# Attention stage of a Mamba-2 and stick-breaking trunk: when the gate, the flips and the transposes run, and on which PSUM banks

## The chip, the cores and the metric

One Trainium2 chip, one core of it. The metric is the time of one execution on the device in microseconds (us), the median of several. Five engines work side by side, each through a queue of its own in order: TensorE (PE in the rows; PEld is its loading of stationary operands), VectorE (DVE), ScalarE (ACT), GpSimd (POOL) and SyncE (SP, which issues the DMAs). Matmuls write to PSUM, eight banks of 512 floats in each of 128 partitions.

## The reference

The reference is a decoder trunk of two layers over 1024 positions of width 1024: a Mamba-2 layer, then a stick-breaking attention layer with 16 heads of 64. The change is in the second layer alone. There the queries, a gate and the shared keys and values are projected, keys and queries are normalised per head, and each block of 128 queries is combined with the keys before it:

```python
z = jnp.einsum('bhtd,bhsd->bhts', q[:, :, q0:kend], k[:, :, :kend])
log_keep = jnp.where(strict, jax.nn.log_sigmoid(-z), 0.0)
suffix = lax.cumsum(log_keep, axis=3, reverse=True) - log_keep
weights = jnp.where(strict, jnp.exp(jax.nn.log_sigmoid(z) + suffix), 0.0)
...
outs.append(jnp.einsum('bhts,bhsd->bhtd', weights, v[:, :, :kend]))
...
return (o * jax.nn.silu(gate)) @ w_out
```

The kernel computes the weights as differences of a running product of sigmoid(-z), which one scan gives, and multiplies them by differences of neighbouring values.

## The kernel before

All large products are made in three passes of a reduced float type: each operand is split in a high half (rounded, by ACT) and a low half (the rest, by DVE or POOL), and high x high, high x low and low x high are added in PSUM.

`attention` goes through 8 head pairs `hp` and, in each, through 4 pairs of 128-row blocks, p = 3, 2, 1, 0: 32 steps, and two more at the end. Positions are stored in reverse, so block pair p = 3 sees the fewest keys and p = 0 the most. Step i mixes three kinds of work:

- **fill** for `steps[i]`: `project` of the blocks 2p+1 and 2p (24 matmuls of 384 columns each: keys, values and queries), and in the steps p = 3 and p = 2 `gate` of one half of the positions (24 matmuls of 512 columns). The generators give way (`yield`) every so many matmuls, and the pieces below are put in there. A list of weights (5, 7, 5) turns the count of yields into a position between 0 and 1.
- **pieces for `steps[i-1]`**: `flip` (L873) transposes its normalised keys and queries into one PSUM bank `tq` (L879) and splits them into `kst`, `qh` and `ql` by ACT and DVE (L885 to L890). Then `scores` makes z for two heads and two blocks (L906, L907), ACT takes sigmoid(-z) (L908), and DVE's scan makes the running product `pt` (L910).
- **pieces for `steps[i-2]`**: `turn` transposes blocks of `pt` (L922, L925) into a `tr` bank and splits them into `wh` (ACT, L931) and `wl` (DVE, L932). `product` multiplies them by the values into `oq` (L942), two turns behind. `fold` reads `oq` by ACT and DVE (L953, L954), adds, and multiplies by the gate `GT` (L959).

So in a step p the pieces are the scores of block pair p+1 and the products of p+2 (of the pair before where that runs over). The number of turns is 6, 8, 2 and 4 in the steps p = 3, 2, 1 and 0; the keys that the scores reach are 896 and 1024, 128 and 256, 384 and 512, 640 and 768.

After the fill of a step come `values` (DMAs on SP that shift the values by one row, then POOL) and `norm` (sum of squares, twelve small DVE operations, one multiply of `kq`). The weights of the next pair are split into halves by ACT and DVE (L104, L108) as soon as their buffers come free. They come free when the last fill of p = 0 has read them.

The order of PE is the order in which the code issues. Only PE is scheduled by hand (`manual_schedule`); the order of the other engines is made by the planner of the framework, which also puts the waits in. The PSUM banks of the stage are `mm` 2, `z` 2, `tr` 2 and `oq` 2. In the last steps `b2.weights` loads the output weights and splits them, the low halves in turn on POOL and DVE. Steps 32 and 33 have as their fill the first output products (`b2.fill`, L1116).

```python
SPREAD = ((0.05, 0.95), (0.62, 1.0))
FLIP = 0.5
...
yield from split3_some(nc, ps[:, :384], prs, 6)
...
fill = [(project(sts[hp], 2 * p + 1), 5)]
if p >= 2:
    fill.append((gate(sts[hp], p - 2), 7))
fill.append((project(sts[hp], 2 * p), 5))
...
for f, w in fill:
    for _ in f:
        done += 1
        while pieces and pieces[0][0] <= done / total:
            pieces.pop(0)[1]()
```

## Time and profile before

| | us |
|---|---|
| median of 3 runs | 1828.4 (1828.0 to 1832.74) |
| the profiled execution | 1827.5 |
| its span, first to last instruction | 1825.8 |
| attention, from its first projection to the first output product | about 654 (927.4 to 1581.8) |

Over the whole span PE is busy 94%, DVE 65%, ACT 49% and POOL 22%. Shares of the span are averages over stages with different limits; in the attention stage DVE is far busier than in the rest. The profile gives each instruction its engine, its line in the kernel, the tiles it writes and reads (out<-in), its shape, start and duration, and where an engine sat idle in front of it, for how long and what ended that. Matmuls are pipelined: the duration of one is longer than the distance to the next, and the distance is what counts.

### The profile page before, as it was taken

How to read it: one execution, taken by the hardware profiler on the slowest of the kernel's cores; microseconds unless marked ns; L12 is line 12 of the kernel's file. 1: busy time of each engine (PE TensorE's matmuls, PEld its weight loads, DVE VectorE, ACT ScalarE, POOL GpSimd, SP SyncE). 2: the span in 40 equal slices, each digit the busy share in tenths (PEclk: the TensorE clock that was granted, in tenths of full speed). 3: DMA queues.
4: the chain of work that ended last, by engine and by line, in shares of the span. 5: the costliest groups of instructions: out<-in, count | busy, mean ns of one | idle time of the engine just before them, and what ended most of it. 6: DMA issues, size and time to landing. Idle time of an engine off the chain costs nothing.

```text
span 1825.8 us, 25280 instructions
## 1 busy us (share of the span) xinstructions
PE 1719.5 (94%) x9170; PEld 1449.3 (79%) x9170; DVE 1186.9 (65%) x2462; ACT 893.0 (49%) x1912; POOL 406.1 (22%) x450
## 2 busy tenths in 40 slices
PE   7999999999999999999998999998999998789999
PEld 6777877877886877888887888887888887677887
DVE  6687278179169645335659787978878787764332
ACT  6567349339337433123436464655646564642121
POOL 0234534624625122210001010111111012211110
PEclk9999999999999999999999999999999999899999
DMA  4222213213212655322211110101101011323110
GB/s 156 66 82 84 90 58 99 87 56 96 102 53 88 218 160 173 104 98 79 83 65 49 37 53 20 54 20 51 43 28 56 29 41 37 122 76 116 51 39 35
DMA packets 96397, 139.42 MB, mean 76 GB/s; under 512 B 18160, under 2 KB 66640, under 8 KB 96272
## 3 DMA queue, kind: packets, MB, share of 16 engines
q1 hardware_dynamic: 96272, 137.80, 23.5%
q8 instruction: 72, 1.18, 0.3%
q14 instruction: 53, 0.43, 0.1%
HBM read 108.77 MB, written 24.77 MB: 73 GB/s over the span
## 4 chain that ended last, share of the span: by engine, by line
PE 69%; DVE 19%; ACT 6%; DMA 3%; issue 2%; POOL 1%; SPq 0%; DVEq 0%; POOLq 0%; ACTq 0%
PE mm L46 37%; PE mm L53 12%; DVE pt L910 6%; PE mm L1116 4%; PE pq L46 2%; PE oq L942 2%; DVE v L234 2%; PE intra L409 2%; DVE g0l L108 1%; PE tr L922 1%; PE inter L404 1%; DVE wl L932 1%; PE tr L664 1%; PE tr L925 1%; PE tr L388 1%
## 5 line engine op out<-in xcount | busy, mean ns | idle before, releaser
L46 PE MATMUL mm<-ul,wh 128*128 128x512 f32 (+1 forms) x648 | 254.0, 392 | 0.0
L46 PE MATMUL mm<-uh,wl 128*128 128x512 f32 (+1 forms) x648 | 252.5, 390 | 0.0
L46 PE MATMUL mm<-uh,wh 128*128 128x512 f32 (+1 forms) x648 | 252.4, 389 | 0.1
L53 PE MATMUL mm<-g0h,hh 128*128 128x384 f32 x512 | 182.7, 357 | 0.0
L910 DVE TENSOR_TENSOR_SCAN pt<-pt,keep 128x128 f32<-128x128 f32 (+7 forms) x128 | 175.8, 1376 | 0.9 <-ACT pt L908 0.3
L53 PE MATMUL mm<-g0l,hh 128*128 128x384 f32 x512 | 172.8, 338 | 2.4 <-DVE g0l L108 2.4
L53 PE MATMUL mm<-g0h,hl 128*128 128x384 f32 x512 | 173.0, 338 | 0.0
L931 ACT CAST wh<-tr 128x512 fp32r<-128x512 f32 (+1 forms) x160 | 86.7, 543 | 165.0 <-PE tr L925 164.3
L234 DVE SCALAR_TENSOR_TENSOR v<-u,convh,v 128x512 f32<-128x512 f32 x144 | 129.4, 904 | 55.1 <-ACT v L232 52.6
L853 POOL TENSOR_TENSOR vs<-vs,vr 128x256 f32<-128x256 f32 x32 | 24.8, 776 | 548.5 <-DMA vs<-vr 265.9
L46 PEld LDWEIGHTS mm<-ul,wh 128*128 128x128 f32 x648 | 121.7, 188 | 26.2 <-issue 2.3
L46 PEld LDWEIGHTS mm<-uh,wh 128*128 128x128 f32 x648 | 121.7, 188 | 25.7 <-issue 1.1
L46 PEld LDWEIGHTS mm<-uh,wl 128*128 128x128 f32 x648 | 121.8, 188 | 25.5 <-issue 1.9
L932 DVE TENSOR_TENSOR wl<-tr,wh 128x512 fp32r<-128x512 f32 (+1 forms) x160 | 101.5, 635 | 55.6 <-ACT wh L931 53.5
L106 POOL TENSOR_TENSOR wl<-raw,wh 128x1024 fp32r<-128x1024 f32 x39 | 95.2, 2441 | 156.2 <-ACT wh L104 156.2
L574 DVE SCALAR_TENSOR_TENSOR acc<-mm,rg,acc 128x512 f32<-128x512 f32 x64 | 47.8, 749 | 84.5 <-PE mm L46 84.0
L53 PEld LDWEIGHTS mm<-g0l,hh 128*128 128x128 f32 x512 | 96.9, 189 | 3.9 <-DVE g0l L108 3.0
L53 PEld LDWEIGHTS mm<-g0h,hh 128*128 128x128 f32 x512 | 96.7, 189 | 1.0
L53 PEld LDWEIGHTS mm<-g0h,hl 128*128 128x128 f32 x512 | 96.4, 188 | 0.0
L922 PE MATMUL tr<-ident,pt 128*128 128x128 f32 x320 | 74.0, 280 | 23.5 <-DVE wl L932 22.3
L906 PE MATMUL z<-kst,qh 128*128 128x320 f32 (+3 forms) x192 | 72.2, 376 | 25.3 <-ACT pt L908 16.4
L908 ACT ACTIVATE pt<-z 128x320 f32<-128x320 f32 (+3 forms) x192 | 89.7, 489 | 8.9 <-PE z L907 7.4
(368 smaller groups left out, 4286.7 us busy)
## 6 DMA issues: line engine op xcount, KB each, us to landing
raw<-in_w_in SPq DMA_DIRECT2D x40, 512.0 KB
ex<-acd SPq DMA_DIRECT2D x64, 256.0 KB
raw<-in_w_b SPq DMA_DIRECT2D x32, 512.0 KB
raw<-in_m_out SPq DMA_DIRECT2D x16, 512.0 KB
raw<-in_gate SPq DMA_DIRECT2D x16, 512.0 KB
graw<-gT SPq DMA_DIRECT2D x30, 256.0 KB
gT<-zs SPq DMA_DIRECT2D x28, 256.0 KB
acc<-in_x SPq DMA_DIRECT2D x8, 512.0 KB
```

The source lines that it names most:

```text
L46: nc.tensor.matmul(out, lhsT=a, rhs=b, start=(i == 0), stop=(i == n - 1))
L53: nc.tensor.matmul(out, lhsT=a, rhs=b, start=(i == 0), stop=(i == n - 1))
L106: (eng or nc.gpsimd).tensor_tensor(lo, raw, hi.bitcast(F32), op=ALU.subtract)
L234: nc.vector.scalar_tensor_tensor(vv, u[:, 3 - j:3 - j + 512], w(j), vv, op0=ALU.mult, op1=ALU.add)
L574: nc.vector.scalar_tensor_tensor(acc[:, sl], ps, k.rg[:, g, t:t + 1], acc[:, sl], op0=ALU.mult, op1=ALU.add)
L906: nc.tensor.matmul(z[:, :n], lhsT=qh[:, h, qs], rhs=rk, start=True, stop=False)
L908: nc.scalar.activation(pt[:, ko:ko + n], z[:, :n], AF.Sigmoid, scale=-1.0)
L910: nc.vector.tensor_tensor_scan(pt[:, :N], pt[:, :N], keep[:, :N], 1.0, op0=ALU.mult, op1=ALU.max)
L922: nc.tensor.transpose(tq[:, c:c + P], al[:, i0:i0 + P], ident)
L931: nc.scalar.copy(wh[:, :c], tq[:, :c])
L932: nc.vector.tensor_tensor(wl[:, :c], tq[:, :c], wh[:, :c].bitcast(F32), op=ALU.subtract)
L1116: nc.tensor.matmul(pss[n], lhsT=a, rhs=b, start=(q == 0 and i == 0), stop=(q == 1 and i == 11))
```

## The change

Six things change, all in `attention` but the last:

- The gate moves from the steps p = 3 and p = 2 to p = 1 (between the two projections) and p = 0 (behind them); in the last pair to p = 2 and p = 1.
- The fill gives way every two matmuls (before: six in a projection, four in a gate), and the weights (12 each) match the number of yields.
- The flip moves from 0.5 to 0.58 of a step, the scores begin at 0.66 for 0.62. The flip writes keys and queries to two banks, and its ACT and DVE operations are put in another order.
- The transposes have three banks, and the products of both heads share one bank `oqs`, 256 columns each, which stays allocated.
- The copy of the values out of PSUM goes from DVE to ACT.
- In `B2.weights` all low halves are made by POOL.

```diff
-SPREAD = ((0.05, 0.95), (0.62, 1.0))
-FLIP = 0.5
+SPREAD = ((0.05, 0.95), (0.66, 1.0))
+GATE = {1: 1, 0: 0}
+GATE7 = {2: 1, 1: 0}
+FLIP = 0.58
...
-        trp = ctx.enter_context(tc.tile_pool(name="b_tr", bufs=2, space=PSUM, reuse_waits="tile"))
-        op = ctx.enter_context(tc.tile_pool(name="b_o", bufs=2, space=PSUM, reuse_waits="tile"))
+        trp = ctx.enter_context(tc.tile_pool(name="b_tr", bufs=3, space=PSUM, reuse_waits="tile"))
+        op = ctx.enter_context(tc.tile_pool(name="b_o", bufs=1, space=PSUM, reuse_waits="tile"))
...
+        oqs = op.tile([P, 512], F32, name="oq")
...
         def project(st, b):
-            yield from split3_some(nc, ps[:, :384], prs, 6)
+            yield from split3_some(nc, ps[:, :384], prs, 2)
...
-            nc.vector.tensor_copy(st["vr"][p][:, b % 2], ps[:, 128:256])
+            nc.scalar.copy(st["vr"][p][:, b % 2], ps[:, 128:256])
...
         def gate(st, half):
-            yield from split3_some(nc, gp, prs, 4)
+            yield from split3_some(nc, gp, prs, 2)
...
         def flip(st, p):
-            tq = trp.tile([P, 512], F32, name="tr")
-            for i in range(2):
-                for m in range(2):
-                    nc.tensor.transpose(tq[:, m * 256 + i * P:m * 256 + (i + 1) * P], kn[:, i, m], ident)
-            kt, qt = tq[:, 0:256], tq[:, 256:512]
+            kt, qt = (trp.tile([P, 512], F32, name="tr")[:, :256] for _ in range(2))
+            for m, t in ((0, kt), (1, qt)):
+                for i in range(2):
+                    nc.tensor.transpose(t[:, i * P:(i + 1) * P], kn[:, i, m], ident)
             qh = wk.tile([P, 2, 256], F32R, name="qh", bufs=1)
             for h in range(2):
+                o = own[h]
+                nc.scalar.activation(kst[o, h, tsl], kt[o], AF.Copy, scale=k.gkq[o])
+            for h in range(2):
                 o, x = own[h], own[1 - h]
-                g = k.gkq[o]
-                nc.scalar.activation(kst[o, h, tsl], kt[o], AF.Copy, scale=g)
                 nc.vector.scalar_tensor_tensor(
-                    kst[x, h, tsl], kt[o], g, kst[o, h, tsl].bitcast(F32), op0=ALU.mult, op1=ALU.subtract)
+                    kst[x, h, tsl], kt[o], k.gkq[o], kst[o, h, tsl].bitcast(F32), op0=ALU.mult, op1=ALU.subtract)
+            for h in range(2):
+                o, x = own[h], own[1 - h]
                 nc.scalar.copy(qh[o, h], qt[o])
                 nc.scalar.copy(qh[x, h], qt[o])
+            for h in range(2):
+                o = own[h]
                 nc.vector.tensor_tensor(ql[o, h], qt[o], qh[o, h].bitcast(F32), op=ALU.subtract)
...
         def product(st, p, h, j0):
-            if j0 == 2 * p:
-                st["oq"] = op.tile([P, 512], F32, name="oq")
-            out = st["oq"][:, :256]
+            out = oqs[:, h * 256:h * 256 + 256]
...
         def fold(st, p, h):
-            hp, GT, oq = st["hp"], st["GT"], st["oq"]
+            hp, GT, oq = st["hp"], st["GT"], oqs[:, h * 256:h * 256 + 256]
...
-                fill = [(project(sts[hp], 2 * p + 1), 5)]
-                if p >= 2:
-                    fill.append((gate(sts[hp], p - 2), 7))
-                fill.append((project(sts[hp], 2 * p), 5))
+                fill = [(project(sts[hp], 2 * p + 1), 12), (project(sts[hp], 2 * p), 12)]
+                half = (GATE if hp < 7 else GATE7).get(p)
+                if half is not None:
+                    fill.insert(2 - half, (gate(sts[hp], half), 12))
...
         def weights(self, kks):
-            k.hilo(hi[:, sl], lo[:, sl], raw.rearrange("p (n c) -> p n c", n=2), eng=k.nc.vector if kk % 2 else None)
+            k.hilo(hi[:, sl], lo[:, sl], raw.rearrange("p (n c) -> p n c", n=2))
```

## Rows read from the trace of the kernel before

**Rows 1.** The page, its chain that ended last: shares of the span by engine.

```profile
PE 69%; DVE 19%; ACT 6%; DMA 3%; issue 2%; POOL 1%; SPq 0%; DVEq 0%; POOLq 0%; ACTq 0%
```

**Rows 2.** Windows of pair 3, p3 to p0: us; busy PE, PEld, DVE, ACT, POOL; clock.

```profile
1156.40:1180.90 24.50, 23.68 (x140) 21.30 (x139) 21.13 (x44) 15.06 (x34) 2.48 (x5) 1.00 0.22 71
1180.90:1206.20 25.30, 22.57 (x147) 20.94 (x146) 18.43 (x39) 10.65 (x25) 2.16 (x5) 1.00 0.02 5
1206.20:1219.30 13.10, 12.58 (x77) 11.77 (x76) 10.19 (x31) 7.37 (x18) 2.10 (x5) 1.00 0.15 52
1219.30:1238.00 18.70, 16.22 (x99) 14.50 (x98) 17.84 (x41) 13.57 (x33) 2.65 (x5) 1.00 0.13 37
```

**Rows 3.** Timeline of PE: start us, duration us, line, operation, out<-in, shape, count.

```profile
1168.25 0.39 PE L53 MATMUL mm<-hl,g0h 128*128 128x512 f32 x1
1168.48 0.27 PE L879 MATMUL tr<-ident,kq 128*128 128x128 f32 x1
...
1222.99 0.27 PE L922 MATMUL tr<-ident,pt 128*128 128x128 f32 x1
1223.10 0.27 PE L925 MATMUL tr<-ident,pt 128*128 128x128 f32 x1
1223.12 0.42 PE L53 MATMUL mm<-g0h,hh 128*128 128x384 f32 x1
```

**Rows 4.** Windows, as rows 2: first pair, next six, then the last pair's steps.

```profile
927.40:990.10 62.70, 59.18 (x339) 54.14 (x338) 42.55 (x114) 32.05 (x75) 7.53 (x15) 1.00 0.08 24
990.10:1483.40 493.30, 453.44 (x2737) 413.54 (x2737) 406.69 (x905) 281.13 (x640) 57.11 (x120) 0.99 0.13 40
1483.40:1534.10 50.70, 47.72 (x286) 43.49 (x286) 36.64 (x73) 23.77 (x51) 5.68 (x11) 0.97 0.08 26
1534.10:1554.40 20.30, 14.29 (x76) 12.91 (x75) 15.60 (x33) 10.00 (x22) 6.20 (x7) 0.92 0.34 120
1554.40:1581.80 27.40, 16.77 (x102) 14.77 (x100) 22.93 (x47) 15.04 (x33) 9.57 (x15) 0.90 0.22 78
```

**Rows 5.** Waits of PE in six pairs: total us, times, longest us.

```profile
PE tr L922 <- DVE wl L932: 19.2, 16, 2.7
PE z L906 <- ACT pt L908: 12.6, 24, 1.1
PE mm L53 <- DVE g0l L108: 2.4, 2, 1.7
```

**Rows 6.** Timeline, start of step p2 of pair 3; idle before and its releaser in brackets.

```profile
1183.95 2.28 DVE L910 TENSOR_TENSOR_SCAN pt<-pt,keep 128x1024 f32<-128x1024 f32 x1
...
1188.10 0.56 DVE L932 TENSOR_TENSOR wl<-tr,wh 128x384 fp32r<-128x384 f32 x1
...
1188.71 0.33 PE L922 MATMUL tr<-ident,pt 128*128 128x128 f32 x1 [2.73 <-DVE wl L932]
```

**Rows 7.** Timeline, a flip and the first scores behind it, step p0 of pair 3.

```profile
1229.82 0.36 ACT L888 CAST qh<-tr 64x256 fp32r<-64x256 f32 x1 [1.09 <-DVE kst L886]
...
1230.61 0.41 PE L906 MATMUL z<-kst,qh 128*128 128x320 f32 x1 [0.82 <-ACT qh L889]
```

**Rows 8.** Groups of DVE by line, six pairs: busy us, mean ns, idle before us.

```profile
L826 DVE COPY vr<-mm 128x128 f32<-128x128 f32 x48 | 13.7, 284 | 2.8 <-ACT kq L825 2.4
L840 DVE TENSOR_TENSOR GT<-mm,sg 128x512 f32<-128x512 f32 x12 | 8.3, 692 | 4.7 <-ACT sg L839 4.7
```

**Rows 9.** Timeline, fold of head 0 in step p2 of pair 4.

```profile
1279.66 0.40 PE L942 MATMUL oq<-wl,V 128*128 128x256 f32 x2
...
1282.07 0.42 DVE L954 TENSOR_TENSOR of<-oq,of 64x256 f32<-64x256 f32 x1
```

**Rows 10.** Timeline, POOL and PE at the first output product.

```profile
1577.94 1.03 POOL L853 TENSOR_TENSOR vs<-vs,vr 128x256 f32<-128x256 f32 x1 [6.67 <-DMA vs<-vr]
...
1581.68 2.37 POOL L106 TENSOR_TENSOR hl<-raw,hh 128x1024 fp32r<-128x1024 f32 x1
...
1581.77 0.80 PE L1116 MATMUL mm<-hh,V 128*128 128x512 f32 x1 [8.14 <-POOL V L106]
```

## The prediction

> **What bounds the kernel now.** I read the page first, then the attention stage step by step, then the waits of the matmul engine, then single stretches. The chain of work that ended last is 69% matmul engine (PE) and 19% vector engine (DVE) [rows 1]; so PE sets the pace, with DVE close behind it somewhere. The table of one head pair by step shows where [rows 2]. Call a step by its block pair: p3, p2, p1, p0. They last 24.5, 25.3, 13.1 and 18.7 us, 81.6 together, and DVE is busy 21.13, 18.43, 10.19 and 17.84 of that: in p0 DVE itself is full (95%).
>
> How long PE would need with no wait comes from the spacing of its matmuls [rows 3]: 512 columns start 0.23 us apart, that is 0.45 ns a column; transposes start 0.11 apart, and the matmul behind the last of a group follows after 0.02. With the column counts of the code: two projections, 48 x 384 columns, 8.3 us; a gate, 24 x 512, 5.5 us; scores 3.5, 0.7, 1.6, 2.5 us for p3, p2, p1, p0; products 2.5, 3.5, 0.7, 1.6; transposes (26, 34, 10, 18 of them in 7, 9, 3, 5 groups) 2.2, 2.9, 0.8, 1.5. PE's floor is then 22.0, 20.9, 11.4 and 13.9 us, 68.2 a pair. Against the larger of PE's floor and DVE's busy time (22.0 + 20.9 + 11.4 + 17.8 = 72.1) a pair loses 81.6 - 72.1 = 9.5 us: 2.5 in p3, 4.4 in p2, 1.7 in p1, 0.9 in p0. The six pairs of the middle take 493.3 us, 82.2 each [rows 4].
>
> Three waits make the loss up [rows 5]. Transposes of the weights wait for the low half of an earlier turn (19.2 us in six pairs). The longest of it sits at the start of p2: scans of 2.28 us still fill DVE, the low half comes at 1188.10, and PE stands 2.73 us [rows 6]. Scores wait for an evacuation by ACT (12.6 us). And the flip is slow: its one bank is read in turn, ACT's copy of q waits 1.09 us for DVE's work on k, though the two read different columns [rows 7].
>
> **The change part by part.**
>
> **Gates.** They leave p3 and p2 (5.5 us of PE each) and go to p1 and p0. PE's floors become 16.5, 15.4, 16.9, 19.4: the same 68.2, and level now. DVE's multiply of the gate, 0.69 us [rows 8], goes along. The value copies (0.284 us, 8 a pair, 0.57 a step [rows 8]) leave DVE for ACT, which is busy 46.7 of 81.6 us and hides them [rows 2]. SP's shift of the values then starts no later than now, for it no longer waits for DVE's queue; on PE only the tail waits for it. DVE becomes 21.13 - 0.57 - 0.69 = 19.9 in p3, 17.2 in p2, 10.3 in p1, 18.0 in p0. The larger of the two, step by step: 19.9 + 17.2 + 16.9 + 19.4 = 73.4. This is no better than the 72.1 of before: **the edit gives nothing by itself and takes PE work away from the two steps in which DVE is behind.** What can be won is part of the 9.5 us.
>
> **Late gate in p0.** The weights of p0 are now let go by the gate, in the last third of the step, so the next pair's halves are made later; DVE does eight of them, and PE waited for such a half twice, 2.4 us in all [rows 5]. Cost between 0 and 1.2 us a pair; I take 0.3, since after the first pair no such wait stands in the rows.
>
> **Third transpose bank.** At the start of p2 the third turn no longer waits, but the product right behind it needs the same low half. The 2.73 us shrink only by what now stands between: one turn (0.35) and a few matmuls, 0.5 to 1.3 us. The flip takes two of the three banks, so in the middle of a step the gain is smaller. Between 0 and 1.3 us a pair; I take 0.8.
>
> **Flip on two banks.** ACT's six copies no longer wait for DVE. The stall behind it is 0.82 us of PE in p0 and the smaller score waits of p1 and p3. It is worth 0.8 to 2 us a pair; I take 1.5. Flip and scores also start later (0.58 and 0.66 of a step for 0.5 and 0.62), so DVE's normalisation has more time ahead of the flip.
>
> **A piece every two matmuls.** Before, a projection yields four times where five were counted, so the last fifth of the pieces came in one lump behind the fill and waited on ACT (12.6 us of score waits in six pairs, 2.1 a pair [rows 5]). Spread out, most of these go: 1.5 us; between 0.5 and 2.1. In return the step's projection ends at its very end, and the normalisation that led during the lump starts later; the flip at 0.58 leaves some 9 us for it.
>
> **One bank for the products of both heads.** Here is the new wait. Head 1's first product goes into the bank from which head 0's fold is still read. In p2 the add that ends the reading ends at 1282.49, 2.4 us after head 0's last product ended at 1280.06 [rows 9]. In the new order the two products are 2.7 slots of 0.35 us and one turn apart, 1.3 us. So PE waits 2.4 - 1.3 = 1.1 us in p2; in the other steps the distance is 1.7 us or more and I count nothing. Bounds 0 and 2.4. That other columns of one bank are kept apart too is what [rows 7] show, so I take 1.1. Behind the waiting product stand the next projection matmuls and turns, PE being in order. The Trainium skill says the same in "PSUM — Partial Sum Buffer", section "PSUM bank collisions raise a hardware error": two engines on one bank and quadrant must be kept apart even at disjoint columns. The trace agrees with its 1.09 us. By that rule the term is 1.1, without it 0, and the sum 6.6 us less for six pairs. The Trainium skill's page "Perfetto Trace Analysis", section "Optimizing Tensor Performance", asks that independent groups rotate through banks, so it speaks against this edit.
>
> **Low halves of the output weights** go from DVE to GpSimd (POOL), 2.37 us each [rows 10]. POOL's queue goes in order, and the last wait of the stage, 8.14 us of PE, is for POOL. But POOL sits idle 6.67 us just before, waiting for the shifted values, and one such half fits there: 0, or 2.4 us if it lands behind. I take 0.6 with the lump gone from this last step.
>
> **The sum.** Loss per pair: p3 keeps 1.2 of 2.5 (score waits gone, DVE now the limit), p2 2.0 of 4.4 (the 1.1 of the shared bank and 0.9 of the old wait), p1 0.6 of 1.7, p0 1.3 of 0.9 (PE and DVE level, and the 0.3 of late weights): 5.1 us. 73.4 + 5.1 = 78.5 a pair, 471.0 for six: **-22.3**. First pair: floors 8.3 + 9.4 + 16.9 + 19.4 = 54.0 and 5 of loss, 59.0 for 62.7: **-3.7**. Last pair [rows 4]: p3 and p2, where the gate stays in p2, 17.3 (DVE) + 20.9 (PE) + 5 = 43.2 for 50.7: -7.5; p1 with a gate in it, 16.9 + 2.5 = 19.4 for 20.3: -0.9; p0 up to the fill 28.0 for 27.4: +0.6. Together **-7.8**. In all -33.8. The profiled execution took 1827.5 us (span 1825.8), 0.9 below the median of 1828.4; so 1793.7 for it, and **1795 us** against the median.
>
> **The rivals.**
>
> Slower: DVE piles up where the gates were. In p3 it has 3.4 us more than PE (19.9 against 16.5). In the trace its scans already run 5.3 us past the start of p2 (1180.9 to 1186.2 [rows 6]); 8.7 with the surplus, 9.3 with the low half. The product that needs that half now sits 3.1 us into p2 (slot 6 and three turns), so PE waits 6.2 us instead of 2.73, and its clock may be held back afterwards: the last pair's p3 and p2, at a granted mean of 0.97, take 50.7 us [rows 4] where those at 1.00 take 49.8 [rows 2], 0.9 more. Then p2 is 15.4 + 6.2 + 1.1 + 0.9 = 23.6, p3 19.9 + 2.5 = 22.4, p1 and p0 16.9 + 1.7 + 19.4 + 0.9 = 38.9: 84.9 a pair, +16 in six, nothing at either end: **1845 us**. It decides from a loss of 82.2 - 73.4 = 8.8 us a pair. For it: the step table. Against: p1, where DVE has 6.6 us to spare, comes right behind.
>
> No change: the waits move and do not shrink. Only PE's order is written out; DVE's is the planner's, and if it goes on taking scans and weight halves ahead of low halves, the loss stays at 9.5, 82.9 a pair, +4 in six and -8 at the ends: about **1824**. For it: a third bank only moves the wait to the next product. Against: flip and lump are cured by PE's order and by banks alone.
>
> More: DVE carries 3 us of its surplus of 5.2 in p3 and p2 into p1, where PE has no need of it. 75 a pair, -43, with -13 at the ends: **1772**. For it: few pieces in p1, so nothing there asks DVE early. Against: a product two turns later asks for each low half.
>
> **How the numbers follow.** My forecast, 1780 to 1815, gets 0.52; below it 0.17; between 1815 and 1823 0.07; no change 0.10; slower 0.14. About 0.3% (5.5 us) is what a measurement here can tell from none: faster 0.76, same 0.10, slower 0.14. The range leaves out 0.06 below 1766 and 0.12 above 1836; it takes in the bounds of the shared bank (0 to 2.4 us, -7 to +8 in six pairs), of the third bank and of the late weights.
>
> **What would show it.** p3 and p2 near 21 and 19 us with DVE over 90% busy, p1 near 17.5, p0 near 20.7; transposes that hardly wait for a low half, and products that do; a product of head 1 that waits for the add of the fold; ACT's copies of q right behind those of k. Wrong if p3 and p2 together stay above 43 us, if p0 waits for weight halves, or if the tail grows by more than 3 us.

## The result and the profile after

The changed kernel takes **1877.4 us** (median; 1874.0 to 1882.8) against 1828.2 us before: a ratio of 1.0267, 95% interval 1.0237 to 1.0297. The forecast was 1795 us, the range 1766 to 1836. The change makes the kernel slower by 49 us, and the prediction was wrong in sign.

The profiled execution took 1882.8 us, its span 1881.1. Five windows of it, on the bounds of [rows 4] (first pair; the next six; the last pair's p3 and p2; its p1; its p0 up to the third output product). Columns: us, busy time of PE, PEld, DVE, ACT and POOL, granted clock, DMA share, GB/s.

```profile
927.80:991.70 63.90, 60.01 (x339) 55.48 (x338) 42.27 (x108) 34.22 (x85) 8.37 (x18) 0.97 0.08 25
991.70:1536.20 544.50, 471.16 (x2738) 434.45 (x2737) 398.64 (x855) 284.51 (x686) 55.28 (x119) 0.94 0.11 36
1536.20:1581.50 45.30, 41.70 (x263) 37.78 (x262) 35.69 (x69) 23.07 (x53) 5.39 (x10) 1.00 0.13 38
1581.50:1604.80 23.30, 19.32 (x100) 17.70 (x99) 17.72 (x33) 12.66 (x28) 12.04 (x9) 0.93 0.39 139
1604.80:1638.90 34.10, 16.88 (x102) 15.05 (x100) 21.02 (x48) 16.35 (x36) 11.20 (x16) 0.84 0.09 26
```

Against [rows 4]: +1.2 in the first pair, **+51.2 in the six pairs** (where -22.3 was forecast), -5.4 in the last pair's p3 and p2, +3.0 in its p1, +6.7 in the tail. The steps of pair 3, to be read against [rows 2]:

```profile
1168.60:1197.70 29.10, 20.52 (x117) 18.41 (x116) 21.86 (x41) 13.93 (x32) 2.25 (x5) 0.88 0.21 73
1197.70:1221.60 23.90, 20.37 (x123) 19.47 (x122) 15.86 (x35) 10.29 (x25) 2.65 (x5) 0.86 0.03 6
1221.60:1239.60 18.00, 17.93 (x101) 16.23 (x100) 12.49 (x32) 8.38 (x22) 2.09 (x5) 1.00 0.11 38
1239.60:1261.10 21.50, 20.69 (x123) 19.08 (x122) 16.34 (x38) 14.79 (x38) 2.54 (x6) 1.00 0.05 12
```

p1 and p0 came out near the forecast (17.5 and 20.7 were named). p3 took 29.1 us instead of 21, p2 23.9 instead of 19. The waits of PE in the six pairs show what fills p3 and p2 (total us, times, longest us; [rows 5] has those of the kernel before):

```profile
PE oq L948 <- issue: 34.5, 6, 6.7
PE oq L948 <- DVE wl L940: 15.4, 12, 1.8
PE oq L948 <- DVE of L960: 10.4, 6, 1.7
PE z L915 <- DVE ql L898: 8.6, 11, 0.8
```

The largest, five stalls of some 6.7 us and one of 1.2 in the first of the six pairs, has no releaser, so the timeline of the stall has to be read engine by engine (step p3 of pair 3; start us, duration, engine, line, operation, then the idle time before it and its releaser). First SP and POOL, then ACT, then PE:

```profile
1160.15 0.64 SPq L851 DMA_DIRECT2D vs<-vr  x1
...
1170.95 0.56 SPq L853 DMA_DIRECT2D vs<-keep  x1
1171.55 12.29 SPq L760 DMA_DIRECT2D raw<-in_w_b  x4
...
1169.87 1.05 POOL L863 TENSOR_TENSOR V<-vs,V 128x128 fp32r<-128x128 f32 x2
...
1175.50 0.51 ACT L106 ACTIVATE g0h<-raw,kvn 128x256 fp32r<-128x256 f32 x1 [7.36 <-DMA raw<-in_w_b]
...
1178.84 1.45 ACT L939 CAST wh<-tr 128x384 fp32r<-128x384 f32 x3
...
1179.42 0.66 PE L948 MATMUL oq<-wh,V 128*128 128x256 f32 x2 [6.62 <-issue]
```

SP's queue holds the zero row for the values of p3 (`vs<-keep`) ahead of the four weight loads of the next pair. The zero row goes into the one buffer `vs`, which POOL reads until 1170.9. So the loads leave at 1171.55, the first lands about 1175.5, and ACT, in order, has stood 7.36 us at the split of that weight. Behind it in ACT's queue stand three more splits, two sigmoids of scores, the gate's sigmoid, the square of the normalisation and three casts `wh`; PE's product needs the first of those casts. In the kernel before two of the four loads stood ahead of the zero row; the same queue there:

```profile
1149.23 0.59 SPq L758 DMA_DIRECT2D raw<-in_w_b  x1
...
1156.56 0.34 SPq L758 DMA_DIRECT2D raw<-in_w_b  x1
...
1165.00 0.57 SPq L849 DMA_DIRECT2D vs<-keep  x1
1165.68 0.51 SPq L758 DMA_DIRECT2D raw<-in_w_b  x1
```

After the stall TensorE runs at its lower level: the granted clock is 1.00 (2.4 GHz) before it and 0.51 (1.2 GHz) right behind it, and full again from 1184 on.

```profile
1168.60:1172.80 4.20, 4.20 (x29) 3.78 (x27) 4.07 (x7) 0.00 (x0) 2.25 (x5) 1.00 0.03 5
1179.40:1184.00 4.60, 3.91 (x14) 3.65 (x15) 4.12 (x14) 1.37 (x3) 0.00 (x0) 0.51 0.00 0
1184.00:1190.00 6.00, 4.70 (x31) 3.77 (x29) 4.27 (x13) 3.80 (x10) 0.00 (x0) 1.00 0.29 88
```

### The profile page after: what moved, and what is told of

Same layout as the page of the kernel before. It is cut to its first block, busy times and chain, and to the rows that moved or that the text cites. A ratio compares the mean times of both kernels' runs of the same rounds, so it can differ in the third digit from the quotient of the medians.

```text
span 1881.1 us, 25474 instructions
## 1 busy us (share of the span) xinstructions
PE 1737.1 (92%) x9170; PEld 1470.6 (78%) x9170; DVE 1177.3 (63%) x2394; ACT 901.4 (48%) x1976; POOL 412.6 (22%) x454
## 3 DMA queue, kind: packets, MB, share of 16 engines
q1 hardware_dynamic: 96272, 137.80, 22.7%
## 4 chain that ended last, share of the span: by engine, by line
PE 69%; DVE 13%; ACT 8%; DMA 5%; issue 2%; POOL 2%; SPq 0%; DVEq 0%; POOLq 0%; ACTq 0%
PE mm L48 35%; PE mm L55 12%; PE mm L1122 4%; PE oq L948 3%; PE pq L48 2%; DMA vs<-vr 2%; DVE pt L918 2%; DVE v L236 2%; PE intra L411 2%; PE z L915 1%; PE tr L930 1%; PE inter L406 1%; ACT qh L895 1%; PE z L914 1%; ACT qh L894 1%
## 5 line engine op out<-in xcount | busy, mean ns | idle before, releaser
L918 DVE TENSOR_TENSOR_SCAN pt<-pt,keep 128x128 f32<-128x128 f32 (+7 forms) x128 | 173.1, 1357 | 19.0 <-ACT pt L916 17.6
L55 PE MATMUL mm<-g0l,hh 128*128 128x384 f32 x512 | 184.4, 360 | 0.0
L55 PE MATMUL mm<-g0h,hl 128*128 128x384 f32 x512 | 183.5, 358 | 0.0
L857 POOL TENSOR_TENSOR vs<-vs,vr 128x256 f32<-128x256 f32 x32 | 24.8, 775 | 598.1 <-DMA vs<-vr 316.1
L48 PEld LDWEIGHTS mm<-uh,wl 128*128 128x128 f32 x648 | 121.8, 188 | 25.5 <-issue 1.9
L48 PEld LDWEIGHTS mm<-uh,wh 128*128 128x128 f32 x648 | 121.7, 188 | 25.5 <-issue 1.1
L916 ACT ACTIVATE pt<-z 128x320 f32<-128x320 f32 (+3 forms) x192 | 94.0, 490 | 67.4 <-PE z L915 66.2
L948 PE MATMUL oq<-wh,V 128*128 128x256 f32 x320 | 65.2, 287 | 46.2 <-issue 34.5
L948 PEld LDWEIGHTS oq<-wh,V 128*128 128x128 f32 x320 | 61.1, 201 | 54.4 <-issue 36.4
L55 PEld LDWEIGHTS mm<-g0l,hh 128*128 128x128 f32 x512 | 101.5, 198 | 2.2
L55 PEld LDWEIGHTS mm<-g0h,hl 128*128 128x128 f32 x512 | 101.1, 198 | 1.6
L55 PEld LDWEIGHTS mm<-g0h,hh 128*128 128x128 f32 x512 | 100.8, 197 | 1.2
L576 DVE SCALAR_TENSOR_TENSOR acc<-mm,rg,acc 128x512 f32<-128x512 f32 x64 | 47.8, 749 | 84.4 <-PE mm L48 83.6
```

The costliest lines, as they stand in the source:

```text
L48: nc.tensor.matmul(out, lhsT=a, rhs=b, start=(i == 0), stop=(i == n - 1))
L55: nc.tensor.matmul(out, lhsT=a, rhs=b, start=(i == 0), stop=(i == n - 1))
L576: nc.vector.scalar_tensor_tensor(acc[:, sl], ps, k.rg[:, g, t:t + 1], acc[:, sl], op0=ALU.mult, op1=ALU.add)
L916: nc.scalar.activation(pt[:, ko:ko + n], z[:, :n], AF.Sigmoid, scale=-1.0)
L918: nc.vector.tensor_tensor_scan(pt[:, :N], pt[:, :N], keep[:, :N], 1.0, op0=ALU.mult, op1=ALU.max)
L948: nc.tensor.matmul(out[:, :w], lhsT=st["V"][j // 2][:, j % 2, h * P:(h + 1) * P], rhs=rhs, start=(j0 == 2 * p and i == 0), stop=(j0 == NT ...
```

## The experiments

**Theory.** The gate that runs last in p0 lets the pair's weights go late; the planner then puts the loads behind the zero row on SP, and ACT's queue carries the delay to PE. **Rivals.** DVE piles up in p3 and p2 (the prediction's rival); the shared product bank; or the move of the gates costs by itself, because the gate's matmuls need nobody and so cover the waits of p3 and p2. All steps below are lengths worked out from the traces in one way, from the first projection matmul of a step to that of the next, mean over the six pairs; "six" is their sum in us, "time" the median. "Last" is the last pair, and "tail" its p0 up to the third output product. A ratio is to the kernel before, run on the same chip.

| kernel | time | six | p3 | p2 | p1 | p0 | last p3+p2 | last p1 | tail |
|---|---|---|---|---|---|---|---|---|---|
| before | 1828.2 | 493.3 | 24.8 | 25.6 | 13.1 | 18.7 | 50.7 | 20.4 | 27.3 |
| after | 1877.4 | 544.5 | 28.6 | 22.7 | 17.9 | 21.5 | 45.2 | 23.3 | 34.1 |
| e3_gates_only | 1878.7 | 544.8 | 25.9 | 24.7 | 17.6 | 22.6 | 47.8 | 21.3 | 29.0 |
| e1_gate_mid | 1854.0 | 517.2 | 25.2 | 21.6 | 17.9 | 21.5 | 45.4 | 22.0 | 32.8 |
| e5_keep_pool | 1852.3 | 514.5 | 24.7 | 21.6 | 17.9 | 21.5 | 45.4 | 24.4 | 33.7 |
| e2_gates_back | 1817.8 | 481.1 | 25.7 | 23.8 | 13.7 | 17.0 | 47.9 | 20.4 | 33.5 |
| e6_gates_p2_p1 | 1848.0 | 512.2 | 25.1 | 24.3 | 18.1 | 17.9 | 45.7 | 24.5 | 33.5 |
| e13_moved_flip_one | 1870.4 | 531.1 | 29.5 | 19.8 | 17.6 | 21.6 | 44.7 | 24.5 | 34.0 |
| e14_moved_flip_one_keep | 1849.4 | 509.2 | 25.1 | 20.6 | 17.6 | 21.6 | 46.0 | 23.3 | 34.4 |
| e4_own_banks | 1875.6 | 533.2 | 26.5 | 22.4 | 17.9 | 22.0 | 51.0 | 23.5 | 34.3 |
| e12_back_own_banks | 1848.6 | 505.2 | 28.0 | 25.1 | 13.8 | 17.4 | 51.2 | 20.1 | 33.6 |
| e11_flip_one | 1807.6 | 473.3 | 24.5 | 23.0 | 13.2 | 18.2 | 46.2 | 21.2 | 33.8 |
| e8_only_fine | 1844.2 | 503.0 | 27.7 | 24.0 | 13.3 | 18.8 | 49.6 | 20.2 | 34.0 |
| e10_back_coarse | 1828.8 | 494.2 | 24.7 | 25.1 | 13.1 | 19.4 | 49.7 | 16.3 | 31.4 |
| e7_back_hl_dve | 1816.5 | 480.3 | 25.6 | 23.8 | 13.7 | 17.0 | 48.0 | 19.8 | 31.2 |
| e9_last_coarse | 1814.6 | 481.2 | 25.7 | 23.8 | 13.7 | 17.0 | 48.0 | 21.7 | 29.0 |
| e15_flip_one_hl_dve | 1805.1 | 473.3 | 24.5 | 23.0 | 13.2 | 18.2 | 46.2 | 20.0 | 31.6 |

### The gates and the queue of the loads

**e3_gates_only**: the kernel before with the gates' new steps and nothing else of the change.

```diff
-if p >= 2:
-    fill.append((gate(sts[hp], p - 2), 7))
...
+half = (GATE if hp < 7 else GATE7).get(p)
+if half is not None:
+    fill.insert(2 - half, (gate(sts[hp], half), 7))
```

> The kernel before with the move of the gates alone (the same steps and the same place in the step as in the changed kernel); yields, flips, banks and copies as before. In the program three weight loads stand behind the zero row on SP. Theory Q: ACT stands at a late weight half in p3 here too, some 5 to 7 us a pair, and the time is 1850 to 1870. Theory D: p3 and p2 show waits for low halves by DVE, not for a load; also 1850 or more. If the move alone costs nothing (1823 to 1835), the loss needs the other edits as well.

Measured 1878.7 us, 1.0284 (1.0267 to 1.0300): the move of the gates alone costs as much as the whole change, and more than the 1850 to 1870 us that were named for the queue alone. The other edits gain and lose about nothing between them when the gates are moved.

**e1_gate_mid**: the changed kernel with the gate always between the two projections, so that a projection is the last reader of the weights.

```diff
-fill.insert(2 - half, (gate(sts[hp], half), 12))
+fill.insert(1, (gate(sts[hp], half), 12))
```

> The changed kernel with one line different: in p0 the gate runs between the two projections, not behind them, so the weights are let go by a projection, as before the change. In the program SP then issues two weight loads ahead of the zero row of the shifted values, where the changed kernel has all four behind it. Theory Q (queue): the 6.6 us that PE stands in p3 of five pairs come from ACT, which stands 7.4 us at a weight half whose load was issued late, because SP sat at the zero row in front of it. Then p3 falls from 29 to 21 to 22 us, ACT's wait for the weight load goes, and the time is 1877 - 5 x 7.5 = about 1840. Theory D (DVE): p3 is long because the gate's matmuls no longer cover DVE's backlog; the gate is still not in p3, so p3 stays above 27 us and the time at 1870 or more.

Measured 1854.0 us, 1.0148 (1.0127 to 1.0168). ACT no longer waits for a load at all, and 27 us of the six pairs come back. The time lies between the two expectations (1840 for the queue alone, 1870 or more for DVE). p3 keeps 25.2 us: its flip now waits up to 3.3 us for the normalised keys and its products for low halves, both from DVE.

**e5_keep_pool**: the changed kernel with the zero row of p3 issued by POOL's queue. PE, DVE and ACT have the same instructions in the same order as in the changed kernel; only the loads stand earlier on SP.

```diff
-nc.sync.dma_start(vs[P - 1:P, 1], st["vr"][p + 1][0:1, 0] if p < 3 else zrow)
+(nc.sync if p < 3 else nc.gpsimd).dma_start(vs[P - 1:P, 1], ...)
```

> The changed kernel with one DMA moved: in step p3 the zero row (vs<-keep) is issued by GpSimd's queue and no longer by SP's. PE, DVE and ACT keep exactly the order of the changed kernel; on SP the four weight loads now stand ahead of the shift of the values. Theory queue: the 6.6 us that PE stands in p3 in five pairs are the four loads waiting on SP behind vs<-keep, which waits for POOL's V of the step before. Then the loads go out some 10 us earlier, the 7.36 us of ACT at g0h<-raw go, p3 falls from 28.6 us to 22 to 25, and the time to 1842 to 1860. Rival DVE pile-up: loads are early and PE waits in p3 for DVE's low halves all the same; p3 stays at 27 or more and the time at 1867 to 1880.

Measured 1852.3 us, 1.0134 (1.0121 to 1.0148), **25 us off by one DMA of 0.5 KB moved to another queue**. The same place in its trace (SP, ACT, PE):

```profile
1159.78 15.05 SPq L760 DMA_DIRECT2D raw<-in_w_b  x4
...
1164.55 0.51 ACT L106 ACTIVATE g0h<-raw,kvn 128x256 fp32r<-128x256 f32 x1 [1.26 <-DMA raw<-in_w_b]
...
1170.10 0.41 PE L948 MATMUL oq<-wh,V 128*128 128x256 f32 x2 [2.15 <-issue]
```

The step starts at 1163.8 here and at 1168.6 in the changed kernel, so the loads begin to leave 4.0 us ahead of its start instead of 2.9 behind it, and PE's stall falls from 6.62 to 2.15 us. What is left of it has a second cause besides the 1.26 us at the load: the square of the normalisation goes into the one buffer `sg`, which DVE's multiply of the gate still reads, and ACT stands there too.

```profile
1169.00 0.63 ACT L868 ACTIVATE sg<-kq 128x512 f32<-128x512 f32 x1 [1.51 <-DVE GT L844]
```

In the six pairs PE's stall of this kind falls from 34.5 us to

```profile
PE oq L948 <- issue: 11.9, 6, 2.2
```

ACT's waits for loads in the six pairs (total us, times, longest us), after:

```profile
ACT g0h L106 <- DMA raw<-in_w_b: 37.3, 6, 7.5
```

and in e5:

```profile
ACT g0h L106 <- DMA raw<-in_w_b: 6.8, 6, 1.3
```

The same line gives 3.3 us before, 36.8 in e3_gates_only and 43.8 in e13 (below), and does not stand among the waits of e1 and e2: the wait follows the order on SP's queue in all of them.

So the queue is worth 30.0 us of the six pairs (544.5 to 514.5). Of these 23.4 lie in p3. The other 6.6 lie in p2, where PE's waits are the same in both and the granted clock falls less often in e5 (last section). It is not all: 514.5 is still 21 above the kernel before.

**e2_gates_back**: the changed kernel with the gates in p3 and p2 again, all other edits kept.

```diff
-half = (GATE if hp < 7 else GATE7).get(p)
+half = p - 2 if p >= 2 else None
...
-fill.insert(2 - half, (gate(sts[hp], half), 12))
+fill.insert(1, (gate(sts[hp], half), 12))
```

> The changed kernel with the gates back in p3 and p2, between the projections, as before the change; all else as changed (fine pieces, flips late and on two banks, three transpose banks, one product bank, value copies on ACT). SP's order is that of e1. Theory Q: with the load in time, what is left of the change is worth the cure of the flip and of the lump, less 1.7 us a pair in p2 for the shared bank: p3 23.5, p2 24, p1 12, p0 16.5, about 76 to 78 a pair, 1800 to 1812 with a tail that is 7 us longer than before. Theory D says that the place of the gates is all the loss: 1877 less 9 us a pair, about 1805 too; but then e1 stays slow. If this one stays above 1850, neither holds.

Measured 1817.8 us, 0.9951 (0.9936 to 0.9966): faster than before, though less than expected. Against e5, where the loads are early too, the six pairs are 33.4 us shorter. The table shows how the move fails step by step, from e2 to e5: taking a gate of 5.5 us out of p3 and p2 shortened them by 1.0 and 2.2 us, putting it into p1 and p0 lengthened those by 4.2 and 4.5.

**e6_gates_p2_p1**: the changed kernel with one gate in p2 and one in p1; p0 has two projections alone.

```diff
-GATE = {1: 1, 0: 0}
+GATE = {2: 1, 1: 0}
```

> The changed kernel with one gate of a pair in p2 and the other in p1 (the last pair already has them there), so p0 has two projections alone and lets go of the pair's weights from the middle of its fill on. Theory queue: SP sends loads ahead of vs<-keep again, p3 is 21 to 23 us, p2 23 to 24, p1 17.9, p0 17 to 17.5: some 80 a pair, 1812 to 1825. Theory that DVE's work per step decides (p3 has 16.5 us of PE and 19.9 of DVE, the difference lands in p2): p3 and p2 together 47 or more, p1 17.9, p0 17.5, 83 or more a pair, 1828 to 1840.

Measured 1848.0 us, 1.0109 (1.0094 to 1.0125), slower than both expectations. The steps add up as above: p2 with a gate and p0 without one are within a microsecond of e2, p1 pays 4.4, and p3 without its gate gives 0.6. In p3 the matmuls that are gone are replaced by waits for DVE: 3.1 us of the flip for the normalised keys and 1.8 of the products for low halves (pair 3; DVE busy 21.6 of 25.5 us). ACT waits for no load here, as in e1; so these two, 31.1 and 36.1 us behind e2 in the six pairs, show the loss without the queue's cause.

**e13_moved_flip_one** and **e14_moved_flip_one_keep** ask whether the flip on two banks, which e11 below shows to be a loss, made the move costly. e13 is the changed kernel with the flip of before; e14 has the zero row on POOL's queue as well.

```diff
-kt, qt = (trp.tile([P, 512], F32, name="tr")[:, :256] for _ in range(2))
+tq = trp.tile([P, 512], F32, name="tr")
...
+kt, qt = tq[:, 0:256], tq[:, 256:512]
```

> The changed kernel with the flip on one bank as before; SP still issues the four weight loads behind vs<-keep. Theory: the queue's loss is separate from the flip's, so PE still stands for late loads in p3 (5 to 7 us in five pairs), and the flip gives what it gave with the gates in place, 7.8 us in six pairs: 537 us and 1866 to 1872. Rival (the two-bank flip makes the move costly): 15 us or more come back, six pairs 530 or less and 1860 or less.

> The changed kernel with the flip on one bank and vs<-keep on GpSimd's queue: both causes found so far are out, the gates stay in p1 and p0. Theory (the gates' move itself costs, for PE loses in p3 and p2 the work that covers waits and gains in p1 and p0 work that covers nothing): p1 17.5 and p0 21.5 to 22.5, p3 and p2 together 43 to 46, six pairs 500 to 514 us and 1838 to 1850. Rival (the flip made the move costly): six pairs 485 or less and 1825 or less.

Measured 1870.4 us, 1.0221 (1.0197 to 1.0246), and 1849.4 us, 1.0110 (1.0074 to 1.0146). In e13 the loads are as late as in the changed kernel (43.8 us of ACT, as said above); the flip gives 13.4 us of the six pairs, more than the 7.8 that it gives with the gates in place. In e14 the six pairs take 509.2 us, against 473.3 in e11, which differs in the place of the gates and the zero row: 35.9 us. The flip is not the cause; **the move of the gates costs 33 to 36 us by itself, whatever the flip.**

What stands in their place is seen in p2. Two lines of PE in e5 (step p2 of pair 3), the only stalls that the timeline marks there, and the DVE lines ahead of the first:

```profile
1190.44 2.28 DVE L918 TENSOR_TENSOR_SCAN pt<-pt,keep 128x1024 f32<-128x1024 f32 x1
1192.64 0.66 DVE L871 TENSOR_REDUCE kss<-sg 128x8 f32<-128x512 f32 x1
1193.33 0.56 DVE L940 TENSOR_TENSOR wl<-tr,wh 128x384 fp32r<-128x384 f32 x1
...
1193.95 0.45 PE L948 MATMUL oq<-wl,V 128*128 128x256 f32 x2 [1.79 <-DVE wl L940]
...
1203.53 0.45 PE L948 MATMUL oq<-wh,V 128*128 128x256 f32 x2 [1.72 <-DVE of L960]
```

The last scans of p3's scores run 4.2 us past the step's start at 1188.5, and the low half comes behind them. In e2 the same two waits in the same step are shorter, for there 24 gate matmuls stand between the pieces:

```profile
1181.78 0.45 PE L948 MATMUL oq<-wl,V 128*128 128x256 f32 x2 [0.26 <-DVE wl L940]
...
1193.80 0.45 PE L948 MATMUL oq<-wh,V 128*128 128x256 f32 x2 [0.69 <-DVE of L960]
```

Against e2 PE's matmuls also run slower: in the six pairs the same 2738 of them are busy 452.4 us at a mean clock of 1.00 in e2, 462.5 at 0.97 in e5 and 471.2 at 0.94 after. So of the 33.4 us between e2 and e5, 10.1 are slower matmuls and 23.3 standing. About half of the standing is the 11.9 us of ACT's stall in p3; e1, where that stall is gone, is no quicker (517.2), for its flips and products wait for DVE instead. That the gate's matmuls hid such waits is read from these steps and waits; no run puts other matmuls in their place.

### Banks, flip and the order of pieces

**e4_own_banks** and **e12_back_own_banks**: two transpose banks and two product banks as before, in the changed kernel and in e2.

```diff
-trp = ctx.enter_context(tc.tile_pool(name="b_tr", bufs=3, ...
-op = ctx.enter_context(tc.tile_pool(name="b_o", bufs=1, ...
+trp = ctx.enter_context(tc.tile_pool(name="b_tr", bufs=2, ...
+op = ctx.enter_context(tc.tile_pool(name="b_o", bufs=2, ...
...
```

> The changed kernel with two transpose banks and a product bank for each head, as before the change. The waits of a product for the fold's add (1.7 us in p2 of each pair) go: 7 x 1.7 = 12 us less, if nothing takes their place. The third bank is lost: the transposes wait for a low half again, up to 2 us a pair. One weight load stands ahead of the zero row on SP and three behind, so theory Q expects ACT's wait to shorten by a load or to stay: 1855 to 1875. A theory that the shared bank is the main loss (product waits are the largest item of PE) expects 1840 or less.

> The kernel of e2_gates_back with two product banks and two transpose banks, as before. By the prediction's terms the shared bank costs 1.1 us a pair and the third bank gives 0.8: 2 us less in six pairs, 1816. In e4_own_banks, where the gates were moved, the same edit took the products' waits away and gave them back as transposes that wait. Rival: with the fine order a turn needs its bank two pieces after the last one, and two banks are too few, as in e8_only_fine (503.0 us): 488 to 498 us and 1825 to 1836.

Measured 1875.6 us, 1.0266 (1.0249 to 1.0283), and 1848.6 us, 1.0112 (1.0099 to 1.0126). With the gates moved, transposes wait where products waited, while the loads are less late (ACT waits 11.0 us for them); the two about cancel. A time of 1840 us or less, named for the shared bank as the main loss, is far off. e4 takes the third bank away as well, so it does not price the shared bank alone; PE's waits for `of` after, 10.4 us in the six pairs, are too few for the main loss. With the gates in place the third bank is worth 24.1 us of the six pairs, net of what the shared product bank costs; even the rival had named no more than 1836 us for e12. The waits of PE in the six pairs of e2:

```profile
PE oq L948 <- DVE wl L940: 6.8, 12, 0.9
...
PE oq L948 <- DVE of L960: 4.1, 6, 0.7
```

and of e12, where the transposes wait instead:

```profile
PE tr L928 <- DVE wl L938: 25.2, 12, 2.7
PE tr L881 <- DVE wl L938: 14.2, 18, 0.9
```

**e11_flip_one**: e2 with the flip of before (the edit of e13).

> The kernel of e2_gates_back with the flip on one bank as before, ACT and DVE in turn for each half. By the prediction's term it is worth 0.8 to 2 us a pair, 1.5 taken: six pairs 481.1 + 9 = 490 (486 to 493), the time 1823 to 1831. Rival: the flip lies beside projection matmuls at 0.58 of a step and its length is hidden: 481 to 484 us and 1817 to 1821.

Measured 1807.6 us, 0.9890 (0.9875 to 0.9905), below both expectations. The flip on two banks is quicker, as predicted (from its first transpose to the first score 2.2 us in e2 and 3.0 in e11, step p0 of pair 3), but a loss: with one bank p0 is 1.2 us longer, and p3, p2 and p1 are 1.2, 0.8 and 0.5 shorter. The first scores of p0 in e2:

```profile
1223.89 0.41 PE L914 MATMUL z<-kst,qh 128*128 128x320 f32 x1
1225.11 0.41 PE L915 MATMUL z<-kst,ql 128*128 128x320 f32 x1 [0.81 <-DVE ql L898]
```

and in e11:

```profile
1220.38 0.41 PE L910 MATMUL z<-kst,qh 128*128 128x320 f32 x1 [0.86 <-ACT qh L893]
1221.05 0.41 PE L911 MATMUL z<-kst,ql 128*128 128x320 f32 x1 [0.26 <-DVE ql L894]
```

With both heads' keys taken first, the first head's low half of q is late by as much as its high half was before: one wait for another. In p3 and p2 the turns share three banks with a flip that holds two; that this is where their 2.0 us lie is argued from the waits and was not tried by itself.

**e8_only_fine**: the kernel before with a piece between every two matmuls and nothing else. **e10_back_coarse**: e2 with the old coarse order.

```diff
-yield from split3_some(nc, ps[:, :384], prs, 6)
+yield from split3_some(nc, ps[:, :384], prs, 2)
...
-fill = [(project(sts[hp], 2 * p + 1), 5)]
+fill = [(project(sts[hp], 2 * p + 1), 12)]
```

> The kernel before with one edit of the change: a piece between every two matmuls of projections and gates, twelve counted for each. By the prediction's term it gives 0.5 to 2.1 us a pair, 1.5 taken: 9 in six pairs and about 2 at the ends, 1815 to 1818. Rival: the edits gain only together (with two transpose banks a finer order makes the turns wait for low halves that come from DVE as late as ever); then 1824 to 1832.

> The kernel of e2_gates_back (gates in p3 and p2; three transpose banks, one product bank, the flip on two banks and later, value copies on ACT) with a piece every six matmuls of a projection and every four of a gate, as before. With the kernel before, e8_only_fine and e2_gates_back it makes a square of two edits: six pairs take 493.3 us with neither, 503.0 with the fine order alone, 481.1 with both. Theory together: the banks and the flip carry the gain and the fine order adds to it only where they are there; then six pairs take 484 to 490 us and the time is 1812 to 1822, the tail 27 to 29. Rival: the banks alone give nothing either (a third bank moves the wait to the product behind it); then 491 to 496 us and 1825 to 1832.

Measured 1844.2 us, 1.0092 (1.0079 to 1.0106), and 1828.8 us, 1.0000 (0.9988 to 1.0013): e8 is slower than both its expectations, e10 is where its rival put it. In six pairs: 493.3 with neither, 503.0 with the fine order alone, 494.2 with the other edits alone (banks, flip, value copies), 481.1 with both. Neither gains without the other. With the fine order the turns come closer together, and with two banks the third has nowhere to go; p3 of e8 (pair 3):

```profile
1167.06 0.33 PE L922 MATMUL tr<-ident,pt 128*128 128x128 f32 x1 [2.63 <-DVE wl L932]
```

### The tail

e8 lengthens the tail from 27.3 to 34.0 us by the fine order alone. POOL and PE at the first output products of e8, to be read against [rows 10]:

```profile
1595.81 0.72 POOL L853 TENSOR_TENSOR vs<-vs,vr 128x256 f32<-128x256 f32 x1 [9.02 <-DMA vs<-vr]
...
1597.91 1.26 POOL L106 TENSOR_TENSOR V<-raw,V 128x512 fp32r<-128x512 f32 x1
...
1590.16 0.79 PE L1116 MATMUL mm<-hh,V 128*128 128x512 f32 x1 [6.95 <-ACT V L104]
...
1599.23 1.22 PE L1116 MATMUL mm<-hh,V 128*128 128x512 f32 x2 [7.85 <-POOL V L106]
```

The last projection matmul starts at 1566.88 before and at 1582.52 in e8, 12.4 and 17.3 us into the step; from there to POOL's V are 14.9 and 16.7 us. Before, a lump of pieces lay beside that chain (shift of the values, POOL's V); in the fine order the pieces lie inside the fill, and PE stands. That this lump was the cover is argued; e9 below tries it.

**e7_back_hl_dve** is e2 with every other low half of the output weights on DVE again; **e9_last_coarse** is e7 with the last step's projections cut as before.

```diff
-k.hilo(hi[:, sl], lo[:, sl], raw.rearrange("p (n c) -> p n c", n=2))
+k.hilo(hi[:, sl], lo[:, sl], raw.rearrange(...), eng=k.nc.vector if kk % 2 else None)
...
+if i == n - 1:
+    fill = [(project(sts[hp], 2 * p + 1, 6), 5), (project(sts[hp], 2 * p, 6), 5)]
```

> The kernel of e2_gates_back (gates back in p3 and p2, all else as changed) with every other low half of the output weights back on DVE. Theory: the tail's 6 us (27.3 before, 33.5 in e2) are POOL's low halves standing ahead of V; then the tail falls to 28 or 29 and the time from 1817.8 to 1812 to 1814. Rival: the tail grows because the last step's products wait for the fold's add on the shared bank and for the flip that comes later; then the tail stays at 32 to 34 and the time at 1816 to 1820.

> The kernel of e7_back_hl_dve with the last step's two projections cut as before (a piece every six matmuls, five counted where four come), so a lump of pieces runs behind its fill again. Theory cover: the tail's growth comes from the fine order of the last step, whose projection ends at its very end, so that the shift of its values (7 us on a queue) and POOL's V have no pieces beside them; in e8_only_fine that edit alone took the tail from 27.3 to 34.0 us. Then the tail falls from 31.2 us to 27 to 28 and the time from 1816.5 to 1811 to 1814. Rival: the flip that comes later sets the tail; then it stays at 30 or more and the time at 1815 to 1818.

Measured 1816.5 us, 0.9938 (0.9926 to 0.9950), and 1814.6 us, 0.9927 (0.9914 to 0.9939). The low halves on POOL are worth 2.3 us of tail (33.5 to 31.2): in e2 one more of 2.34 us stands ahead of V in POOL's queue. The coarse last step takes another 2.2 off the tail, but p1 ahead of it is 1.9 longer, so the lump gives back little by itself: p1 and tail together take 51.0 us in e7 and 50.7 in e9. With the coarse order in every step (e10) they take 47.7, as before the change (47.7), against 53.9 in e2 and 54.2 in e8. The fine order costs these 6 us, then, but not by the lump of the last step alone; how the steps ahead of it have a part in it stays open.

**e15_flip_one_hl_dve** takes out each edit that loses: gates back, flip on one bank, low halves on DVE.

> The kernel of e11_flip_one (gates back, flip on one bank) with every other low half of the output weights back on DVE. The two edits touch different stretches, so their gains should add: six pairs 473, the tail 31 to 32 instead of 33.8, the time 1805 to 1807. Rival: the low halves on DVE push the last pair's flips and nothing is left: 1807 to 1809.

Measured **1805.1 us**, 0.9867 (0.9846 to 0.9887): faster than the kernel before by 1.3%, and the gains add (the six pairs stay at 473.3, the tail falls from 33.8 to 31.6). What is left of the change is the fine order, three transpose banks, the one product bank, the later flip and scores, and the value copies on ACT. Its six pairs run at full clock:

```profile
989.30:1462.50 473.20, 451.03 (x2737) 410.90 (x2736) 399.04 (x857) 287.76 (x686) 60.71 (x120) 1.00 0.15 42
```

## Why the prediction was wrong, point by point

**Gates, on SP's queue: the first step that failed.** The text said that SP's shift of the values starts no later than now, and stopped there. It asked what stands ahead of the shift and not what stands behind it. Behind it stand the four weight loads, in an order that the planner makes, and the late gate changed that order. "Late gate in p0" was given 0 to 1.2 us a pair, 0.3 taken, for PE waiting on weight halves in p0. The cost was 5.0 us a pair (30.0 in six), 3.9 of it in p3, through SP, ACT and a product, and the rest in p2 by the clock, with the weight halves themselves never awaited by PE. That the planner orders all engines but PE was said under "No change" and not drawn on here.

**Gates, as a sum of floors: the second step that failed.** The sum took each step as the larger of PE's floor and DVE's busy time and let the loss fall from 9.5 to 5.1 us a pair. The terms that it priced give only 2.4 of these 4.4 us (0.8 + 1.5 + 1.5 - 1.1 - 0.3); the other 2.0, 12 us in six pairs, stand in no term. With the queue's cause out, e5 has 85.7 us a pair. Its floors by the prediction's recipe are 21.7 (DVE) + 15.7 (DVE) + 16.9 + 19.4 = 73.7, near the 73.4 of the forecast; so the loss is 12.0, of which 3.0 lie in p3 and 5.9 in p2, where 1.2 and 2.0 were allowed (2.0 of the 3.0 are the stall of ACT that is left in e5). The floor was right, and the loss grew where it was to shrink: with the gate's matmuls gone from p3 and p2, waits that they had hidden stood in the open. The text had the sign of it in hand ("takes PE work away from the two steps in which DVE is behind") and priced it at nothing in the sum. In p3 DVE did not become lighter either: 21.9 us busy for 19.9 expected, for the gate's multiply from p0 fell there (0.7 us) and the scans took 0.2 more; the rest is not traced to a line.

**The rival "DVE piles up"** named the place (scans running past the start of p2, a low half behind them) and, with 84.9 us a pair and 1845 us, nearly the time of the kernel without the queue's cause (85.7 and 1852). Its mechanism holds in part: the scans run 4.2 us past the start where 8.7 were named, PE waits 1.8 us there for 6.2, and the rest lies in other waits and in the clock; that the number is so near is in part luck. It was given too small a chance, and the queue had no rival at all.

**p1 and p0** were right: 17.9 and 21.5 us for 17.5 and 20.7.

**Third bank and shared bank** were mis-sized. Together they were to cost 0.3 us a pair (0.8 gained, 1.1 lost); with the gates in place they give 4.0 (e12 to e2). The shared bank's wait is there, 1.7 us after and 0.7 with the gates back, for 1.1. The Trainium skill's "PSUM — Partial Sum Buffer", section "PSUM bank collisions raise a hardware error", which the prediction weighed, has two engines kept apart on one bank even at different columns; the waits for `of` agree with it. The third bank was held to move its wait to the next product; under a fine order it removes 39.4 us of waiting transposes (25.2 + 14.2 in e12) for 10.9 of waiting products.

**Flip on two banks** had the wrong sign: 1.5 us a pair to gain, 1.3 lost (e11 to e2). Its gain was sized from p0, where it is real (1.2 us); p3, p2 and p1 pay 2.5.

**A piece every two matmuls**: 1.5 us a pair to gain. Alone it costs 1.6, on top of the banks it gives 2.2. It was priced as if it stood by itself.

**The tail** was to grow by 0.6 and grew by 6.7 us, and the fine order alone does that (27.3 to 34.0 in e8). The text saw that a step's projection would end at its very end, and asked what that does to the flip, not to the last step's values; by what path the 6 us arise is open in part (e9 and e10 above). Of POOL's low halves it asked the right question (0 or 2.4; 2.3 measured). The last pair's p3 and p2 took 45.2 for 43.2, its p1 23.3 for 19.4, the first pair 63.9 for 59.0.

All three signs named for "wrong" were the right things to look at: p3 and p2 together took 51.3 us for the bound of 43, the tail grew by more than 3; only the wait for weights showed on ACT in p3, not on PE in p0. And the sum for six pairs, -22.3, is close to what the edits give without the gates' move and the two-bank flip (e15: -20.0), but by other terms than those that it was made of.

## What to carry to other kernels

A step that is moved changes the order of every queue that a planner fills for it: for each DMA on such a queue ask what stands behind it, which buffer it waits for, and which engine will stand in order behind the transfer that comes late. Matmuls that wait for nobody are cover: before they are moved to a step with few waits, price the waits that they hide, step by step; here 5.5 us of gate taken out of p3 or p2 gave back 1.0 or 2.2, and put into p1 or p0 cost 4.2 or 4.5. Edits that remove neighbouring waits (a finer order, one more bank) are not a sum of terms: measure or argue them together.

## What the runs showed of the hardware

One DMA of 0.5 KB on SP's queue, waiting for a buffer, held back the four loads of 512 KB behind it, the first by some 7 us and the others by 2 to 6 (by the starts of step p3 in the changed kernel and e5, pair 3); here a queue of DMAs stood at a wait as an engine does.

TensorE's granted clock falls behind some of its waits, short ones too, and not behind others of the same length. After the stall of 6.62 us it was 0.51 for the next 4.6 us. Step p2 of the changed kernel has the same two waits, of 1.8 and 1.7 us, in each of the six pairs. It takes 24 us at a mean clock of 0.86 in pairs 3 and 5, counted from 0 (the window of pair 3 stands above), 22.4 at 0.92 in pairs 1, 4 and 6, and 21 at 1.00 in pair 2. Pairs 4 and 2:

```profile
1290.90:1313.30 22.40, 18.87 (x124) 18.01 (x123) 15.78 (x35) 10.35 (x26) 2.54 (x5) 0.92 0.03 7
1108.30:1129.20 20.90, 17.34 (x124) 16.53 (x123) 15.84 (x36) 10.37 (x26) 2.65 (x5) 1.00 0.03 8
```

e5, with the same two waits, has three pairs at 1.00 and three at 0.92. What decides between them no run here shows.

With the gates in p3 and p2 (e2, e11, e15) and no wait of PE above 1.5 us there, the clock of the six pairs is 1.00 throughout. So the same 2738 matmuls are busy 452.4 us in e2 and 471.2 after: 18.8 us, some 3 a pair, go with TensorE at its lower level. The prediction had 0.9 a pair for it, in one rival only.
